# Attention logits written with their sign turned and a running minimum carried along, and the modulation rows placed under the last query tiles

## The chip, the cores and the metric

One core of a Trainium2 chip runs the whole kernel. The metric is the device time of one execution in microseconds (us), from the first to the last instruction with what lies around it. The engines are named as the profile names them: PE (matrix multiply) and PEld (its weight loads), DVE (the vector engine), ACT (the scalar engine), POOL (GpSimd) and SP (the queue that issues nearly all DMAs). Each engine works through its own queue in order.

## The reference, cut to what matters

One transformer block over 2048 tokens of width 1024. The change lies in the attention, which picks 256 keys for each query by a score and takes a softmax over them:

```
score = sum over 8 index heads of relu(qi . ki) * wi      # per query and key
idx   = top_k(score, 256)                                 # the threshold search
logits = (qa . ckv[idx]) * scale ;  p = softmax(logits) ;  ctx = p . ckv[idx]   # 8 heads
```

and in the modulation rows, which only the layers behind the attention need:

```
mod = silu(c) @ mod_w + mod_b      # c: 1 x 1024, mod_w: 1024 x 6144
sh1, sc1, g1, sh2, sc2, g2 = split(mod)
x = x + g1 * mix ;  h = rmsnorm(x) * (1 + sc2) + sh2 ;  x = x + g2 * moe(h)
```

## The kernel before

The kernel runs as stages: projections (to about 470 us of the profiled execution), attention (about 470 to 1157 us), the output product with the router, and the experts.

**Attention** (`attention`, from line 755) goes over 16 query tiles of 128 queries in the order written in `ORDER`: 0, 1, 2, 6, 7, ... 15, 5, 4, 3. I call them t0, t1, ... by the tile's own number. Tile t looks at (t+1)*128 keys. `p` is the place in that order: p = 4 is t7, p = 10 is t13, p = 12 is t15, p = 13 is t5. A tile has four groups g of two heads. For every (tile, group) `weave` interleaves five generators: `context` of this group (transposes of the exponentials, L1051, and products with the values, L1038), `logits` of the next group (L1012 to L1018), `scores` of the tile three places on (L846 to L850), and the `threshold` searches of the tiles one and two places on (L906 to L954). t5, t4 and t3 have nothing three places on, so the scores end with the work of p = 12. Behind this emission a list scheduler sets each engine's final order, so what stands on an engine is read from the built program.

**Logits** (L1002 to L1018 before): for one head the keys are cut in blocks of 512; PE makes a block in a PSUM bank (`pl`, three buffers), DVE adds the mask while it copies it out to `L` and writes the block's maximum to a column of `st` (one custom instruction and a small read of the accumulator, both L1013). When all blocks of the head are out, a DVE reduction over the one to four maxima gives the negated maximum (L1017), and ACT takes the exponential with it as bias (L1018). `st` is called `ast` in the profile.

**Modulation rows** (`modrows`, from line 169) are 64 steps of DVE work, one 128x512 piece of `mod_w` each, 256 KB, loaded by SP into a tile with two buffers:

```
w = mp.tile([128, 512], F32, name="modr", tag="modr", bufs=2)
with self.tc.issue_after(self.last.ins):
    nc.sync.dma_start(w, self.a["mod_w"][0, k * 128:(k + 1) * 128, o:o + 512])
if k == 0:
    nc.vector.tensor_scalar(acc, w, self.cond[:, 0:1], None, op0=OP.mult)          # L180
else:
    nc.vector.scalar_tensor_tensor(acc, w, self.cond[:, k:k + 1], acc, ...)        # L182
yield
```

`self.last` is the latest load of queries or keys, so a piece is issued behind it on SP. After every eighth piece come a product with ones on PE (L187, into a `pl` bank), an addition (L188) and a small store; that step yields too, so there are 72 steps. A piece's load can only be issued when the DVE step two pieces earlier has given its buffer back. `advance(rows, n)` takes n steps after a (tile, group), at a lowered priority. The layers behind the attention read the rows back from DRAM.

Of the kernel before, what the change touches and what calls it, by code (L numbers as in the profile page):

```python
# [15 lines left out]
AF = mybir.ActivationFunctionType  # L16
OP = mybir.AluOpType
AX = mybir.AxisListType
# [29 lines left out]
class K:  # L48
# [706 lines left out]
    def attention(self):  # L755
        nc, tc = self.nc, self.tc
        with ExitStack() as c1:
            ap = self.ap = c1.enter_context(tc.tile_pool(name="att", bufs=1, reuse_waits="tile"))
            self.pa = c1.enter_context(tc.tile_pool(name="pa", bufs=1, reuse_waits="tile", space=PSUM))
            self.exps = {}  # L760
            rows = self.modrows(ap)
            order = self.ORDER
            groups = [(t, g) for t in order for g in range(4)]
            thr = {}

            def scores(i):

                if i < NT and order[i] >= 3:
                    t = order[i]
                    S = self.ats.tile([128, T], F32, name="S", tag="S", bufs=3)  # L770
                    thr[i] = self.threshold(t, S)
                    return self.scores(t, S), 8 * -(-(t + 1) // 4)
                return iter(()), 0

            def bound(i):

                if i < NT and order[i] < 2:
                    self.plain(order[i])
                return thr.get(i, iter(()))
            for _ in bound(0), bound(1):  # L780
                pass
            for _ in self.logits(*groups[0]):
                pass
            for i, (t, g) in enumerate(groups):
                p = i // 4
                if g == 0:
                    sc, ns = scores(p + 3)
                    b1 = bound(p + 1) if p else iter(())
                    b2 = bound(p + 2)
                na = 2 * -(-(groups[i + 1][0] + 1) // 4) + 1 if i + 1 < len(groups) else 0  # L790
                nx = self.logits(*groups[i + 1]) if na else iter(())
                if g == 3:
                    for _ in b1:
                        pass
                self.weave((self.context(t, g), -(-(t + 1) // 2) + 1 + (g == 3)), (nx, na), (sc, ns // 4 + (g < ns % 4)),
                           (b1, 2), (b2, 1 + g % 2))
                if p >= 4:
                    with tc.high_priority(offset=-100):
                        self.advance(rows, 2)
                if g == 3:  # L800
                    self.advance(sc, 1000)
            for _ in rows:
                pass
            mix = [self.ats.tile([128, KT, 256], F32R, name="S", tag="S", bufs=3) for _ in range(2)]
            self.mix0 = self.mixed(0, mix, [ap.tile([128, 512], F32R, name="rel", tag="rel", bufs=3) for _ in range(2)],
                                   ap.tile([128, 4, 256], F32, name="cj", tag="cj", bufs=2),
                                   lambda: self.bank("pi", 2, (128, 2, 256)))
            self.W = [self.w_cut(self.w_load(k, ap), self.ats, *tag) for k, tag in enumerate((("S", 3), ("R", 1)))]
            raw = [self.w_load(k, ap) for k in range(2, 4)]
            self.repair()  # L810
            self.W += [self.w_cut(w, self.ats, "L", self.LB) for w in raw]
# [176 lines left out]
    def logits(self, t, g):  # L988

        nc, ap = self.nc, self.ap  # L990
        n = (t + 1) * 128
        bias = self.masks[t]
        c, o = t // 4, (t % 4) * 128
        if g == 0:
            self.st = ap.tile([128, 64], F32, name="ast", tag="ast", bufs=2)
        st = self.st
        q = ap.tile([128, 2, 2, 128], F32R, name="qa", tag="qa", bufs=3)
        for r in (slice(0, 64), slice(64, 128)):
            self.last = nc.sync.dma_start(q[r].bitcast(F32), self.qa_d[c][:, g, :, :, o:o + 128])
        P = [self.ats.tile([128, T], F32, name="L", tag="L", bufs=self.LB) for _ in range(2)]  # L1000
        self.exps[t, g] = P, st
        nb = -(-n // 512)  # L1002
        for h in (2 * g, 2 * g + 1):
            L = P[h % 2]
            k = ap.tile([128, T], F32R, name="kc", tag="kc", bufs=3)
            self.last = nc.sync.dma_start(k[:, :n].bitcast(F32), self.kh_d[g][h % 2].rearrange("l d t -> (l d) t")[:, :n])
            mx = st[:, 4 * h:4 * h + nb]
            for i, s in enumerate(range(0, n, 512)):
                e = min(s + 512, n)
                ps = self.bank("pl", 3)  # L1010
                for m in range(2):
                    nc.tensor.matmul(ps[:, :e - s], q[:, h % 2, m], k[:, s:e], start=m == 0, stop=m == 1)  # L1012
                nc.vector.tensor_tensor_reduce(L[:, s:e], ps[:, :e - s], bias[:, s:e], 1.0, -3e38,  # L1013
                                               OP.add, OP.max, mx[:, i:i + 1])
                yield
            neg = st[:, 32 + h:33 + h]
            nc.vector.tensor_reduce(neg, mx, axis=AX.X, op=OP.max, negate=True)  # L1017
            nc.scalar.activation(L[:, :n], L[:, :n], AF.Exp, bias=neg, accum_out=st[:, 40 + h:41 + h])  # L1018

    LB = 4  # L1020

# [791 lines left out]
```

## Time and profile before

| | |
|---|---|
| median of 3 runs | 2235.54 us (2231.49 to 2246.32) |
| the profiled execution | 2253.14 us, its span 2251.3 us |
| mean granted TensorE clock in it | 0.954 |
| busy in it: PE, DVE, ACT, POOL | 2007.1, 1611.3, 1219.2, 906.3 us |
| attention, first logits to the last tile's output | 470 to 1157 us |

The profiled execution took 0.8% longer than the median of the timed runs. Busy time is summed over stages with different limits; what the change touches is read in the attention alone, tile by tile. A tile's end is the DVE instruction at L1070 that writes its output.

### The profile page before, as it was taken

How to read it: one execution, taken by the hardware profiler on the slowest of the kernel's cores; microseconds unless marked ns; L12 is line 12 of the kernel's file. 1: busy time of each engine (PE TensorE's matmuls, PEld its weight loads, DVE VectorE, ACT ScalarE, POOL GpSimd, SP SyncE). 2: the span in 40 equal slices, each digit the busy share in tenths (PEclk: the TensorE clock that was granted, in tenths of full speed). 3: DMA queues.
4: the chain of work that ended last, by engine and by line, in shares of the span. 5: the costliest groups of instructions: out<-in, count | busy, mean ns of one | idle time of the engine just before them, and what ended most of it. 6: DMA issues, size and time to landing. Idle time of an engine off the chain costs nothing. (4 is left out here: it accounts for less than half of the span.)

```text
span 2251.3 us, 37139 instructions
## 1 busy us (share of the span) xinstructions
PE 2007.1 (89%) x12583; PEld 1509.5 (67%) x12584; DVE 1611.3 (72%) x3064; ACT 1219.2 (54%) x2026; POOL 906.3 (40%) x1586
## 2 busy tenths in 40 slices
PE   5899999987888999888979997699999999999983
PEld 4777887855666776776767785466776666666762
DVE  5696899678899989887435555567776676766583
ACT  4832332267777877776642221455665565655552
POOL 4542112537555434375000112334554554555343
PEclk9999999998999999999999998799999999999997
DMA  8737979865777766778877436599999999999894
GB/s 287 261 118 233 275 222 288 265 191 169 240 222 244 232 210 223 223 233 280 235 217 258 144 129 219 177 321 332 349 310 312 292 351 318 340 319 318 302 321 142
DMA packets 317038, 569.61 MB, mean 253 GB/s; under 512 B 35041, under 2 KB 148114, under 8 KB 315812
## 3 DMA queue, kind: packets, MB, share of 16 engines
q1 hardware_dynamic: 292068, 489.26, 66.1%
q0 software_dynamic: 22304, 68.41, 10.6%
q10 hardware_dynamic: 2464, 9.44, 1.1%
q8 instruction: 103, 1.69, 0.3%
q14 instruction: 99, 0.81, 0.1%
HBM read 462.44 MB, written 103.53 MB: 251 GB/s over the span
## 5 line engine op out<-in xcount | busy, mean ns | idle before, releaser
L1645 DVE TENSOR_TENSOR wl<-wr,wh 128x1024 fp32r<-128x1024 f32 x314 | 393.1, 1289 | 173.1 <-ACT wh L1644 172.3
L1644 ACT ACTIVATE wh<-wr 128x1024 fp32r<-128x1024 f32 x372 | 373.7, 1053 | 248.6 <-PE acc L94 182.9
L93 PE MATMUL acc<-wl,xh 128*128 128x512 f32 (+3 forms) x544 | 218.7, 403 | 5.4 <-POOL wl L1645 3.5
L92 PE MATMUL acc<-wh,xh 128*128 128x512 f32 (+3 forms) x544 | 215.9, 407 | 6.7 <-ACT wh L1644 5.0
L1013 DVE CUSTOM_DVE_ANT_0 L<-pl,bias 128x512 f32<-128x512 f32 (+3 forms) x312 | 180.8, 605 | 51.0 <-PE pt L1051 25.5
L94 PE MATMUL acc<-wh,xl 128*128 128x512 f32 (+3 forms) x544 | 215.6, 400 | 0.0
L1012 PE MATMUL pl<-kc,qa 128*128 128x512 f32 (+3 forms) x640 | 188.6, 398 | 25.3 <-DVE ast L1013 12.2
L1051 PE MATMUL pt<-identr,L 128*128 128x128 f32 x1088 | 174.6, 286 | 25.3 <-ACT pT L1053 19.0
L1053 ACT ACTIVATE pT<-pt 128x512 f32<-128x512 f32 (+1 forms) x288 | 158.4, 576 | 64.6 <-PE pt L1051 63.7
L849 ACT ACTIVATE rel<-pi 128x512 f32<-128x512 f32 (+3 forms) x296 | 155.5, 549 | 49.8 <-PE pi L847 23.2
L1645 POOL TENSOR_TENSOR wl<-wr,wh 128x1024 fp32r<-128x1024 f32 x58 | 145.7, 2560 | 90.9 <-ACT wh L1644 88.2
L850 DVE SCALAR_TENSOR_TENSOR S<-rel,wi,S 128x512 f32<-128x512 f32 (+3 forms) x259 | 171.3, 680 | 9.5 <-ACT rel L849 9.3
L611 DVE SCALAR_TENSOR_TENSOR ac<-u,kc,ac 128x512 f32<-128x512 f32 x240 | 175.4, 772 | 0.1
L1051 PEld LDWEIGHTS pt<-identr,L 128*128 128x128 f32 x1088 | 127.5, 144 | 69.4 <-ACT pT L1053 31.1
L1018 ACT ACTIVATE L<-L,ast 128x128 f32<-128x128 f32 (+15 forms) x128 | 154.2, 1207 | 18.5 <-DVE ast L1017 18.1
L1038 PE MATMUL po<-pT,vc 128*64 128x128 f32 x2176 | 150.7, 287 | 7.1 <-ACT pT L1053 6.8
L846 PE MATMUL pi<-kk,qi 128*128 128x512 f32 (+3 forms) x296 | 129.7, 440 | 27.4 <-ACT rel L849 27.0
L1038 PEld LDWEIGHTS po<-pT,vc 128*64 128x64 f32 x2176 | 124.7, 142 | 36.7 <-ACT pT L1053 17.8
L1012 PEld LDWEIGHTS pl<-kc,qa 128*128 128x128 f32 x640 | 110.6, 198 | 57.1 <-DVE ast L1013 24.7
L1695 POOL DMA_INDIRECT x_d<-yo,ent x32 | 93.1, 2910 | 92.6 <-DVE yo L1738 70.6
L92 PEld LDWEIGHTS acc<-wh,xh 128*128 128x128 f32 (+3 forms) x544 | 97.6, 182 | 43.8 <-ACT wh L1644 10.4
L93 PEld LDWEIGHTS acc<-wl,xh 128*128 128x128 f32 (+3 forms) x544 | 99.2, 182 | 37.3 <-POOL wl L1645 4.3
(525 smaller groups left out, 4688.7 us busy)
## 6 DMA issues: line engine op xcount, KB each, us to landing
wr<-in_exp_w_dram SPq DMA_DIRECT2D x256, 512.0 KB
wr<-in_exp_w_dram SPq DMA_DIRECT2D x64, 1024.0 KB
h<-h_d SPq DMA_DIRECT2D x64, 512.0 KB
vc<-v_d SPq DMA_DIRECT2D x112, 256.0 KB
h_d<-h POOLq DMA_DIRECT2D x32, 512.0 KB
qa<-qa_d SPq DMA_DIRECT2D x128, 128.0 KB
modr<-in_mod_w_dram SPq DMA_DIRECT2D x64, 256.0 KB
xt<-in_x_dram SPq DMA_DIRECT2D x16, 512.0 KB
```

The costliest lines, as they stand in the source:

```text
L92: mm(out, lh, rh, start=start, stop=False)
L93: mm(out, lh, rl, start=False, stop=False)
L94: mm(out, ll, rh, start=False, stop=stop)
L611: nc.vector.scalar_tensor_tensor(acc[j], src, kc[:, j, i:i + 1], acc[j], op0=OP.mult, op1=OP.add)
L850: nc.vector.scalar_tensor_tensor(S[:, s:e], r[:, :e - s], self.wi[:, t, h:h + 1], S[:, s:e] if h else self.tie[:, s:e], op0=OP.mult, op1=O ...
L1012: nc.tensor.matmul(ps[:, :e - s], q[:, h % 2, m], k[:, s:e], start=m == 0, stop=m == 1)
L1013: nc.vector.tensor_tensor_reduce(L[:, s:e], ps[:, :e - s], bias[:, s:e], 1.0, -3e38, OP.add, OP.max, mx[:, i:i + 1])
L1038: nc.tensor.matmul(po[r], v[:, (k2 + i) % 4, r], pT[:, i, j], start=len(left) > 2 * t, stop=len(left) <= 2)
L1051: nc.tensor.transpose(pt[:, i, j], P[j][:, (k2 + i) * 128:(k2 + i + 1) * 128], self.ident)
L1053: nc.scalar.activation(pT[:, :m], pt[:, :m], AF.Copy)
L1644: nc.scalar.activation(H[:, s], W[:, s], AF.Copy)
L1645: (nc.gpsimd if pool else nc.vector).tensor_tensor(L[:, s], W[:, s], H[:, s].bitcast(F32), OP.subtract)
```

## The change

Two edits. In `logits`, a block is written negated (factor -1), each block's minimum is started from the column of the block before in place of a constant, and so the last column holds the negated maximum of all the head's blocks; the reduction at L1017 is gone and the exponential turns the sign back with its scale. In `attention`, the modulation rows start at p = 10 (t13) in place of p = 4 (t7), with five steps after each group in place of two: 72 steps over 15 groups in place of 36.

```diff
-                if p >= 4:
+                if p >= 10:
                     with tc.high_priority(offset=-100):
-                        self.advance(rows, 2)
+                        self.advance(rows, 5)
...
-            mx = st[:, 4 * h:4 * h + nb]
             for i, s in enumerate(range(0, n, 512)):
                 e = min(s + 512, n)
                 ps = self.bank("pl", 3)
                 for m in range(2):
                     nc.tensor.matmul(ps[:, :e - s], q[:, h % 2, m], k[:, s:e], start=m == 0, stop=m == 1)
-                nc.vector.tensor_tensor_reduce(L[:, s:e], ps[:, :e - s], bias[:, s:e], 1.0, -3e38,
-                                               OP.add, OP.max, mx[:, i:i + 1])
+                low = st[:, 4 * h + i:4 * h + i + 1]
+                nc.vector.tensor_tensor_reduce(L[:, s:e], ps[:, :e - s], bias[:, s:e], -1.0,
+                                               st[:, 4 * h + i - 1:4 * h + i] if i else 3e38,
+                                               OP.add, OP.min, low)
                 yield
-            neg = st[:, 32 + h:33 + h]
-            nc.vector.tensor_reduce(neg, mx, axis=AX.X, op=OP.max, negate=True)
-            nc.scalar.activation(L[:, :n], L[:, :n], AF.Exp, bias=neg, accum_out=st[:, 40 + h:41 + h])
+            nc.scalar.activation(L[:, :n], L[:, :n], AF.Exp, scale=-1.0, bias=low, accum_out=st[:, 40 + h:41 + h])
```

The two edits also change what the scheduler puts where. Behind line 1007 the lines of the changed kernel are one lower (L1012 is L1011, L1070 is L1069); the DVE instruction of the logits is L1013 in both. The three places that the prediction speaks of follow.

DVE in the middle of the attention, in t8, before: the block of a head, the read of its accumulator (`ISA ast`), and the reduction L1017.

```order
L1013 ISA L,ast<-pl,bias 128x512 [waits PE_49]
L1013 ISA ast 128x1
L850 SCALAR_TENSOR_TENSOR S<-rel,wi,S 128x512 [waits Activation_49] x2
L950 SCALAR_TENSOR_TENSOR bias,sc<-S,sc,nbig 128x1280 [waits DVE_49]
L1017 TENSOR_REDUCE ast<-ast 128x1 [waits DVE_49]
L1013 ISA L,ast<-pl,bias 128x128 [waits PE_49]
L1013 ISA ast 128x1
```

The same engine at nearly the same place in the changed kernel:

```order
L1013 ISA L,ast<-pl,bias,ast 128x512 [waits DVE_49]
L1013 ISA ast 128x1
L1013 ISA L,ast<-pl,bias,ast 128x256 [waits DVE_49,PE_49]
L1013 ISA ast 128x1
L942 SCALAR_TENSOR_TENSOR R<-S,sc,R 128x1408 [waits Activation_49]
L1013 ISA L,ast<-pl,bias 128x512 [waits PE_49]
L1013 ISA ast 128x1
```

The reductions are gone, and a block after the first reads `ast` and waits for DVE itself, here right behind the read that writes it.

DVE in t15, before: pieces of the modulation rows (L182) between blocks of logits.

```order
L1013 ISA L,ast<-pl,bias 128x512
L1013 ISA ast 128x1
L947 TENSOR_TENSOR sc<-sc 128x1
L182 SCALAR_TENSOR_TENSOR macc<-modr,cond,macc 128x512 x2
L1013 ISA L,ast<-pl,bias 128x512
L1013 ISA ast 128x1
L1017 TENSOR_REDUCE ast<-ast 128x1
L1013 ISA L,ast<-pl,bias 128x512
L1013 ISA ast 128x1
L1013 ISA L,ast<-pl,bias 128x512
L1013 ISA ast 128x1
L1013 ISA L,ast<-pl,bias 128x512
```

The same engine in t15 in the changed kernel:

```order
L180 TENSOR_SCALAR macc<-modr,cond 128x512
L192 SCALAR_TENSOR_TENSOR mrow<-mrow,mg 1x512
L182 SCALAR_TENSOR_TENSOR macc<-modr,cond,macc 128x512
L1013 ISA L,ast<-pl,bias 128x512
L1013 ISA ast 128x1
L1013 ISA L,ast<-pl,bias,ast 128x512
L1013 ISA ast 128x1
L182 SCALAR_TENSOR_TENSOR macc<-modr,cond,macc 128x512
L1013 ISA L,ast<-pl,bias,ast 128x512
L1013 ISA ast 128x1
L182 SCALAR_TENSOR_TENSOR macc<-modr,cond,macc 128x512
L1013 ISA L,ast<-pl,bias,ast 128x512
```

Between the outputs of t14 and t15 stand 22 pieces in place of 5, often one or two blocks of logits apart.

SP at the start of t15's loads (rows of 2048 keys), before: keys (kc), values (vc), queries (qa) and the pieces (modr).

```order
L1006 DMA kc<-kh_d_71 128x2048 [waits DMAHW3_49,PE_49]
L178 DMA modr<-in_mod_w_dram 128x512 [waits DMAHW4_49,DVE_49]
L1006 DMA kc<-kh_d_72 128x2048 [waits DMAHW5_49,PE_49]
L999 DMA qa<-qa_d_70 64x4x128 [waits DMAHW6_49]
L999 DMA qa<-qa_d_70 64x4x128 [waits DMAHW7_49]
L1047 DMA vc<-v_d 128x512 [waits DMAHW0_49,PE_49]
L1047 DMA vc<-v_d 128x384 [waits DMAHW1_49,PE_49]
```

The same queue at the same loads in the changed kernel:

```order
L1006 DMA kc<-kh_d_71 128x2048 [waits PE_49]
L178 DMA modr<-in_mod_w_dram 128x512 [waits DMAHW7_49,DMAHW0_49,DVE_49]
L178 DMA modr<-in_mod_w_dram 128x512 [waits DMAHW3_49,DVE_49]
L1046 DMA vc<-v_d 128x512 [waits DMAHW1_49,PE_49]
L1046 DMA vc<-v_d 128x384 [waits DMAHW2_49,PE_49]
L178 DMA modr<-in_mod_w_dram 128x512 [waits DMAHW7_49,DVE_49]
L1006 DMA kc<-kh_d_72 128x2048 [waits DMAHW4_49,PE_49]
L178 DMA modr<-in_mod_w_dram 128x512 [waits DMAHW5_49,DMAHW0_49,DVE_49]
L999 DMA qa<-qa_d_70 64x4x128 [waits DMAHW6_49]
```

Four pieces stand where one stood, each with a wait for DVE, and the next keys and queries are queued behind them.

## Rows read from the trace of the kernel before

**Rows 1.** The page: span, busy time by engine, and the DMA issues of the pieces.
```profile
span 2251.3 us, 37139 instructions
...
PE 2007.1 (89%) x12583; PEld 1509.5 (67%) x12584; DVE 1611.3 (72%) x3064; ACT 1219.2 (54%) x2026; POOL 906.3 (40%) x1586
...
modr<-in_mod_w_dram SPq DMA_DIRECT2D x64, 256.0 KB
```

**Rows 2.** Windows by tile, t6 to t15, then t5: length, busy by engine, clock, DMA.
```profile
523.20:587.50 64.30, 49.72 (x300) 37.17 (x300) 54.38 (x138) 43.86 (x87) 38.33 (x131) 0.87 0.65 190
587.50:631.60 44.10, 36.96 (x269) 29.23 (x270) 35.79 (x88) 30.76 (x56) 24.69 (x78) 0.92 0.61 188
631.60:684.00 52.40, 45.50 (x331) 32.84 (x330) 47.50 (x121) 39.67 (x72) 27.45 (x78) 1.00 0.78 248
684.00:728.90 44.90, 41.44 (x335) 32.07 (x332) 42.10 (x102) 31.93 (x59) 24.56 (x73) 1.00 0.73 233
728.90:784.00 55.10, 50.83 (x384) 39.22 (x385) 49.38 (x115) 45.71 (x79) 24.68 (x76) 0.97 0.76 235
784.00:847.40 63.40, 58.24 (x419) 43.35 (x417) 54.81 (x124) 47.44 (x80) 23.91 (x67) 0.95 0.70 217
847.40:909.70 62.30, 56.93 (x433) 43.55 (x433) 58.10 (x134) 48.26 (x79) 28.59 (x79) 0.97 0.68 214
909.70:978.30 68.60, 60.02 (x477) 48.01 (x477) 60.48 (x144) 50.77 (x84) 32.29 (x115) 0.95 0.75 233
978.30:1044.60 66.30, 57.02 (x467) 44.79 (x465) 53.27 (x145) 48.45 (x80) 45.62 (x173) 0.95 0.73 233
1044.60:1097.40 52.80, 47.01 (x442) 37.10 (x442) 31.82 (x99) 36.99 (x56) 9.03 (x39) 0.97 0.86 276
1097.40:1121.40 24.00, 21.16 (x185) 16.94 (x183) 9.38 (x43) 15.21 (x31) 0.00 (x0) 0.93 0.88 235
```

**Rows 3.** Groups by form, attention: count, busy, mean ns of one, idle before.
```profile
L1013 DVE CUSTOM_DVE_ANT_0 L<-pl,bias 128x512 f32<-128x512 f32 x224 | 148.6, 684 | 40.4 <-PE pt L1051 25.5 <-PE pl L1012 14.5
...
L850 DVE SCALAR_TENSOR_TENSOR S<-rel,wi,S 128x512 f32<-128x512 f32 x196 | 144.2, 745 | 7.7 <-ACT rel L849 7.5
...
L182 DVE SCALAR_TENSOR_TENSOR macc<-modr,cond,macc 128x512 f32<-128x512 f32 x56 | 41.8, 747 | 22.0 <-DMA modr<-in_mod_w_dram 21.8
...
L1017 DVE TENSOR_REDUCE ast<-ast 128x1 f32<-128x4 f32 x32 | 4.8, 149 | 0.1
```

**Rows 4.** DVE timeline, one reduction: start, duration, instruction.
```profile
477.20 0.15 DVE L1017 TENSOR_REDUCE ast<-ast 128x1 f32<-128x1 f32 x1
477.26 0.61 DVE L850 SCALAR_TENSOR_TENSOR S<-rel,wi,S 128x384 f32<-128x384 f32 x1
```

**Rows 5.** DVE timeline, three small instructions, each reading the one before.
```profile
1077.92 0.15 DVE L952 TENSOR_SCALAR sc<-sc 128x1 f32<-128x1 f32 x1
1078.11 0.16 DVE L953 TENSOR_TENSOR sc<-sc 128x1 f32<-128x1 f32 x1
1078.31 0.15 DVE L954 TENSOR_SCALAR bad<-sc 128x1 f32<-128x1 f32 x1
```

**Rows 6.** Waits in the attention: who for whom, us, times, longest.
```profile
ACT L L1018 <- DVE ast L1017: 18.1, 27, 1.9
```

**Rows 7.** Timeline of pieces: SP's issue, DVE's step, in brackets its wait.
```profile
707.65 0.75 DVE L182 SCALAR_TENSOR_TENSOR macc<-modr,cond,macc 128x512 f32<-128x512 f32 x1 [0.25 <-DMA modr<-in_mod_w_dram]
...
713.33 0.85 SPq L178 DMA_DIRECT2D modr<-in_mod_w_dram  x2
720.43 0.75 DVE L182 SCALAR_TENSOR_TENSOR macc<-modr,cond,macc 128x512 f32<-128x512 f32 x1 [2.55 <-DMA modr<-in_mod_w_dram]
...
923.86 1.04 SPq L178 DMA_DIRECT2D modr<-in_mod_w_dram  x1
932.58 0.75 DVE L182 SCALAR_TENSOR_TENSOR macc<-modr,cond,macc 128x512 f32<-128x512 f32 x1 [2.83 <-DMA modr<-in_mod_w_dram]
...
1070.59 0.38 SPq L178 DMA_DIRECT2D modr<-in_mod_w_dram  x1
1075.06 0.75 DVE L182 SCALAR_TENSOR_TENSOR macc<-modr,cond,macc 128x512 f32<-128x512 f32 x1 [1.44 <-DMA modr<-in_mod_w_dram]
```

## The prediction

> **What bounds the kernel now.** I read the page first: PE is busy for 89% of the span and DVE for 72% [rows 1], which says little, since DVE's share is an average over stages. Then I cut the attention at the outputs of the tiles [rows 2]. There both are full: DVE 94% and PE 92% in t9, 90% and 92% in t10, 93% and 91% in t12. In t9 DVE has no time left at all: 42.10 us of work, and 0.25 + 2.55 us in which it stood waiting for a piece of the modulation rows [rows 7], make 44.9 of the window's 44.90 us. In t13 DVE is busy for 60.48 of 68.60 us, in t14 for 53.27 of 66.30. In t15 it falls to 31.82 of 52.80 us, because no scores are left to make. So DVE has room in t15, and the change moves work there. The third view is the timeline of the pieces, which shows how long a load takes from its issue on SP to the step on DVE that waited for it [rows 7].
>
> A measurement of this kernel tells about 1% (22 us) from no change.
>
> **The running minimum.** It removes 128 reductions, 32 of each of four forms, 149 ns each for the largest [rows 3]. Instructions overlap: the next one starts 0.06 us after a reduction [rows 4], so what DVE gets back is 128 x 0.06 = 8 us. It adds no instruction. It makes 192 of the 320 blocks (one per head in t4 to t7, two in t8 to t11, three in t12 to t15) read a column of `ast` that the block before wrote, and wait for it. In the changed order 25 of the 192 stand directly behind that write; for them the trace has three small instructions that each read the one before: they start 0.19 and 0.20 us apart [rows 5] where an independent one follows after 0.06 [rows 4], so 25 x 0.13 = 3 us. For the others the write is over long before. Reading a per-partition operand in place of a constant is not in the trace for this instruction. One bound is nothing; the other is the gap between L850, which has such an operand, and L1013, which has none, at 128x512: 745 - 684 = 61 ns, 192 x 0.061 = 12 us. I take the second, since it comes from the two rows most alike. The first edit's DVE sum is then -8 + 3 + 12 = +7 us, at best -5, spread over 13 tiles.
>
> The Trainium skill ("VectorE: DVE Perf Modes", The DRAIN you can't avoid) says that chained DVE instructions pay nothing for a semaphore, since the next one starts only when the pipe is empty anyway. Rows 4 and 5 differ: dependent small instructions stand 0.13 us further apart. By that rule the 3 us would be nothing.
>
> The exponential can now start one reduction earlier. ACT waited 18.1 us in 27 cases for that reduction [rows 6], but ACT is busy for only 71 to 83% in t8 to t14 [rows 2] and has slack, so I count no time for it; the far bound is a gain of 8 us if half of those waits held PE up. The -1 scale is an operand of an instruction that stays: nothing.
>
> **Pieces out of t6 to t12.** Between the outputs, the changed order has no piece in t6 to t11, 3 in t12, then 19, 16 and 22 in t13, t14 and t15 and 4 in t5. Before there were 7 in most tiles and 5 in t15. A step costs DVE 0.747 us by itself [rows 3], 0.66 from its start to the next one's. I counted the DVE rows of each tile in both orders, each at its distance to the next start in the trace. The difference per tile, moved threshold passes and reductions included, is t6 -7.3, t7 0, t8 -9.0, t9 -4.2, t10 -4.5, t11 -4.5, t12 +2.5, t13 +14.5, t14 -4.3, t15 +7.0, t5 +2.8 us. In t6 to t11 the waits for pieces go too, most of the 22.0 us of rows 3.
>
> What is late next there is PE. Its idle time in t6 to t11 is 324.2 - 282.7 = 41.5 us [rows 2], 14.6 of it in t6, 7.1 in t7, 6.9 in t8 and 3.5 to 5.2 in each of t9 to t11. At a PE share of 92%, the best of these tiles, t7 would give 3.9 us and t8 2.9, and t9 to t11 nothing; at 96% the sum over t7 to t11 is 17 us. The middle of the two is 12. t6 starts the pipeline of thresholds; at 96% it would give 12 us, and I take 4, since its wait is for that pipeline and not for pieces (3 of them). That makes **-16**, between -8 and -28. t12 takes three pieces and another threshold pass: +2.
>
> **Pieces into t13 to t15.** Here I forecast a loss, for two reasons.
>
> First, t13 becomes full. Its DVE work grows to 60.5 + 14.5 = 75 us, 19 pieces wait 22.0 / 56 = 0.39 us each [rows 3], 7.4 us, and 25 carried blocks cost 1.5: 84 us against 68.6. DVE works in order, so nothing shortens that: +15. In t14 work leaves: DVE falls to 49 us, PE loses 7 us of score products, and t14 becomes 61 in place of 66.3: -5.
>
> Second, two buffers set a pace. A piece can be issued when the step two before it is done. From issue to the waiting step it takes 4.5 us at the shortest and 8.7 at the longest [rows 7]; piece 713.33 took 7.1. I take the middle, 6.6. Two pieces then need 6.6 + 0.7 = 7.3 us. Before, the pieces came 6 to 9 us apart each, so this bound nothing. In t15 there are now 22, 11 pairs: 11 x 7.3 = **80 us against 52.8**, +27. While DVE stands at a piece, the blocks of logits behind it on DVE wait, PE waits for their three banks, and ACT for the exponentials. t14's 8 pairs need 58 us, within its 61. On SP the same pieces wait for DVE with the next keys, values and queries queued behind them. t15 moves 276 GB/s at a DMA share of 0.86 already [rows 2]; 17 more pieces of 256 KB [rows 1] are 4.5 MB, 16 us at that rate, so a shorter latency there is not to be expected. t5 takes the last four: +2, and the rows' products on PE (16 of them) move along at no net cost.
>
> The give-back is +2 + 15 - 5 + 27 + 2 = +41; with -16, **+25 us**. On the profiled execution that is 2253 + 25 = 2278, 1.1% more; on the median 2235.5 x 1.011 = **2260 us**.
>
> **The rivals.**
>
> *The loads land fast enough.* Issued more often, a piece may land as quickly as the shortest, 4.5 us; pairs need 5.2 us and t15 11 x 5.2 = 57: +4 in place of +27. t13's waits shrink by half, +11, and t14 keeps -8. The give-back is +2 + 11 - 8 + 4 = +9, the net -7: 2253 - 7 on the profiled execution, **2228 us** on the median. The point is where the give-back is 16: with t13 and t14 as here t15 may then take 64 us, 5.8 a pair, a latency of 5.1 us in t15; below that the kernel is not slower. For it: the shortest row is in t15 itself. Against it: that piece was issued alone, and pieces behind a load of keys took 6 to 9.
> The Trainium skill ("DMA: Bandwidth & Descriptors", Anatomy of one DMA) fits 2.0 us plus the bytes at 436 GB/s for loads issued from GpSimd: by that page 256 KB is an estimated 2.6 us, and the pace would bind nowhere. The rows of this case, issued from SP among other loads, show none under 4.5.
>
> *DVE's relief pays in full.* If DVE alone held t6 to t11 and the waits at pieces were on the path, the gain is 28 us, and with fast loads the net is -19: 2235.5 - 19 = **2216**, and some us lower if the exponentials' earlier start counts. For it: t9's account of DVE, full to the last 0.1 us. Against: at the same time PE is busy for 92%.
>
> *Both ends bad.* No gain beyond t7 and t8 (-8), the pace at 8 us a pair (t15 11 x 8 = 88, +35; t14 8 x 8 = 64, -2), SP held at pieces so that keys come late: +2 + 15 - 2 + 35 + 3 = +53, net +45: **2280 us**. For it: four pieces between the loads of two heads. PE idle may also cost clock: the lowest granted clock of rows 2 to t14, 0.87, a mean of its two levels of 1.2 and 2.4 GHz, stands beside the lowest PE share. That stays in the range.
>
> **How the numbers follow.** The forecast has a chance of 0.46, the fast loads 0.25, both ends bad 0.19, the full relief 0.10. The likeliest case alone spans 2246 to 2276 (latency 6 to 7.2, gain 10 to 22). The range of 8 in 10 leaves out most of the full relief and what lies beyond the bad case: 2222 to 2290. Slower by over 1% is above 2258: six tenths of the forecast, the bad case and a little, 0.49. Faster by over 1% is below 2213: the lower half of the full relief and a little of the fast loads, 0.08. Within 1% is the rest, 0.43.
>
> **What would show it.** In the changed profile the windows between outputs should show t8 and t7 shorter by some 3 to 5 us, t9 to t11 nearly as long, t13 near 84, t14 near 61 and t15 near 80. DVE's idle time at L182 behind `modr` should rise from 22 us to over 50, nearly all after the output of t12, with 6 to 8 us from issue to step. The reductions are gone from DVE and the 128x512 block stands at about 745 ns, or at 684 if the operand is free. I am wrong if t15 stays under 60 us: then the pace of two buffers was no limit. I am wrong in the other term if t6 to t11 lose more than 28 us.

## The result and the profile after

The changed kernel takes **2262.01 us** (median of 7 runs, 2255.51 to 2265.1) against 2235.54 (median of 7, 2231.49 to 2246.32): a ratio of **1.0108, 95% interval 1.0085 to 1.0131**. The forecast was 2260. Where the time went agrees with the forecast in some places, and for the first edit it does not; the experiments show which.

The windows of the changed kernel between the outputs of the tiles, t6 to t15 in turn, with the columns of [rows 2]:

```profile
527.05:583.67 56.62, 46.64 (x292) 35.80 (x292) 48.30 (x118) 39.57 (x79) 36.96 (x128) 0.88 0.59 170
583.67:624.57 40.90, 34.48 (x274) 28.31 (x275) 36.42 (x82) 34.58 (x65) 22.66 (x81) 0.98 0.72 214
624.57:671.26 46.69, 42.21 (x320) 32.40 (x319) 40.03 (x92) 37.41 (x67) 22.71 (x78) 0.98 0.65 204
671.26:716.30 45.04, 42.22 (x341) 33.29 (x341) 39.93 (x95) 34.98 (x64) 22.04 (x78) 1.00 0.66 204
716.30:767.86 51.56, 49.45 (x385) 38.72 (x383) 46.31 (x98) 44.62 (x82) 19.36 (x67) 1.00 0.69 215
767.86:823.81 55.95, 52.94 (x411) 40.92 (x409) 51.11 (x108) 47.04 (x79) 24.70 (x81) 1.00 0.65 199
823.81:895.46 71.65, 61.57 (x450) 47.09 (x448) 63.02 (x124) 53.20 (x88) 28.66 (x88) 0.95 0.60 192
895.46:983.91 88.45, 70.64 (x491) 53.82 (x491) 76.29 (x169) 58.07 (x98) 53.49 (x173) 0.88 0.68 207
983.91:1047.99 64.08, 53.80 (x437) 40.84 (x437) 50.76 (x134) 38.08 (x60) 33.41 (x131) 0.92 0.88 291
1047.99:1117.03 69.04, 55.04 (x458) 40.79 (x456) 40.85 (x96) 36.12 (x56) 0.00 (x0) 0.95 0.88 272
```

Against [rows 2], t6 to t11 are shorter by 27.4 us together, and t12 to t15 are longer by 9.4, 19.8, -2.2 and 16.2. With the small tiles the attention grows by 17.8 us (704.2 against 686.4 from the first logits to the last output), yet the two profiled executions differ by only 9: behind the attention the one of before took 9.7 us longer. Stretches of the stage behind it, before:

```profile
1256.10:1306.10 50.00, 47.66 (x416) 37.89 (x409) 25.03 (x57) 10.54 (x20) 7.43 (x9) 0.93 0.34 117
```

and after, as far behind its last output:

```profile
1274.70:1324.70 50.00, 50.00 (x490) 40.36 (x489) 30.07 (x65) 13.76 (x26) 9.43 (x11) 1.00 0.41 138
```

PE was granted 0.93 there before, a mean of its two levels 1.2 and 2.4 GHz, and 1.00 after, the upper level, in a stretch in which it was busy without a gap. The profiled execution of before, 2253.14 us, is longer than each of the kernel's 7 timed runs and than its 13 runs beside the first four experiments (2221.73 to 2248.64 us); it lies 17.6 us above the median, while the one after is the median itself. That is why the medians differ by more than the two profiles. Where the other executions of before save those 17.6 us isn't shown. Experiment 6, whose DVE order is that of before, was profiled in a long execution too (2253.5 us at a median of 2243.39), with nearly the same attention (682.8 us).

The logits and the pieces of the changed kernel, grouped by form:

```profile
L1013 DVE CUSTOM_DVE_ANT_0 L<-pl,bias,ast 128x512 f32<-128x512 f32 x120 | 89.4, 745 | 3.6 <-PE pl L1011 1.7
L1013 DVE CUSTOM_DVE_ANT_0 L<-pl,bias 128x512 f32<-128x512 f32 x104 | 70.5, 686 | 21.2 <-PE pt L1050 16.1 <-PE pl L1011 4.8
L182 DVE SCALAR_TENSOR_TENSOR macc<-modr,cond,macc 128x512 f32<-128x512 f32 x56 | 41.9, 749 | 30.2 <-DMA modr<-in_mod_w_dram 29.9
L188 DVE TENSOR_TENSOR mrow<-mrow,pl 1x512 f32<-1x512 f32 x8 | 5.4, 671 | 8.5 <-DMA mrow<-in_mod_b_dram 7.3 <-PE pl L187 1.2
L180 DVE TENSOR_SCALAR macc<-modr,cond 128x512 f32<-128x512 f32 x8 | 3.9, 490 | 10.6 <-DMA modr<-in_mod_w_dram 10.6
```

A block that reads the column takes 745 ns, one that doesn't 686. DVE waited 40.5 us for pieces (29.9 at L182 and 10.6 at L180), against 26.0 before (21.8 [rows 3] and 4.2), and once 7.3 us for the bias row behind them.

What DVE waits for in t15, after (us in total, times, longest):

```profile
DVE macc L182 <- DMA modr<-in_mod_w_dram: 12.0, 11, 2.8
DVE mrow L188 <- DMA mrow<-in_mod_b_dram: 7.3, 1, 7.3
DVE macc L180 <- DMA modr<-in_mod_w_dram: 6.8, 2, 5.0
```

And the pace of two buffers in the timeline of t15, first SP's issues of pieces, then DVE's steps (start, duration; in brackets the wait):

```profile
1075.55 0.33 SPq L178 DMA_DIRECT2D modr<-in_mod_w_dram  x1
1079.03 3.18 SPq L178 DMA_DIRECT2D modr<-in_mod_w_dram  x2
...
1074.77 0.75 DVE L182 SCALAR_TENSOR_TENSOR macc<-modr,cond,macc 128x512 f32<-128x512 f32 x1
1078.25 0.75 DVE L182 SCALAR_TENSOR_TENSOR macc<-modr,cond,macc 128x512 f32<-128x512 f32 x1 [1.15 <-DMA modr<-in_mod_w_dram]
1081.10 0.75 DVE L182 SCALAR_TENSOR_TENSOR macc<-modr,cond,macc 128x512 f32<-128x512 f32 x1 [2.10 <-DMA modr<-in_mod_w_dram]
1084.71 0.75 DVE L182 SCALAR_TENSOR_TENSOR macc<-modr,cond,macc 128x512 f32<-128x512 f32 x1 [0.66 <-DMA modr<-in_mod_w_dram]
```

The step at 1074.77 gives its buffer back, the next issue is at 1075.55, its step at 1081.10, 5.6 us later; the step at 1078.25, the issue at 1079.03, the step at 1084.71.

### The profile page after: what moved, and what is told of

It is laid out like the page before. It is cut to its first block, busy times and chain, and to the rows that moved or that the text cites. A ratio compares the mean times of both kernels' runs of the same rounds, so it can differ in the third digit from the quotient of the medians.

```text
span 2260.3 us, 37151 instructions
## 1 busy us (share of the span) xinstructions
PE 2004.4 (89%) x12583; PEld 1507.4 (67%) x12584; DVE 1618.5 (72%) x2936; ACT 1217.3 (54%) x2026; POOL 884.2 (39%) x1586
## 3 DMA queue, kind: packets, MB, share of 16 engines
q1 hardware_dynamic: 292068, 489.26, 65.7%
## 5 line engine op out<-in xcount | busy, mean ns | idle before, releaser
L1011 PE MATMUL pl<-kc,qa 128*128 128x512 f32 (+3 forms) x640 | 194.4, 402 | 30.0 <-DVE ast L1013 19.2
L850 DVE SCALAR_TENSOR_TENSOR S<-rel,wi,S 128x512 f32<-128x512 f32 (+3 forms) x259 | 171.0, 681 | 18.1 <-ACT rel L849 17.9
L1017 ACT ACTIVATE L<-L,ast 128x128 f32<-128x128 f32 (+15 forms) x128 | 154.3, 1207 | 40.9 <-DVE ast L1013 40.0
L1011 PEld LDWEIGHTS pl<-kc,qa 128*128 128x128 f32 x640 | 109.9, 199 | 64.8 <-DVE ast L1013 34.4
L1013 DVE CUSTOM_DVE_ANT_0 L<-pl,bias,ast 128x512 f32<-128x512 f32 (+3 forms) x192 | 123.3, 645 | 7.6 <-PE pl L1011 4.9
L92 PEld LDWEIGHTS acc<-wh,xh 128*128 128x128 f32 (+3 forms) x544 | 97.4, 182 | 43.8 <-ACT wh L1643 10.2
```

Source lines behind the costliest of these rows:

```text
L92: mm(out, lh, rh, start=start, stop=False)
L850: nc.vector.scalar_tensor_tensor(S[:, s:e], r[:, :e - s], self.wi[:, t, h:h + 1], S[:, s:e] if h else self.tie[:, s:e], op0=OP.mult, op1=O ...
```

## The experiments

P is the theory of the prediction: the place of the rows makes the loss. C puts it on the carried minimum, D on DVE's work and not the loads. Ratios are to the kernel before, in runs on the same chip.

**1. The carried minimum alone.** The kernel before with the second part of the diff only; the rows keep `if p >= 4` and two steps.

> The kernel before with the negated logits and the running minimum alone; the modulation rows stay where they were, from t7 on, two steps a group. Theory P (the place of the rows makes the loss): the operand read from a column costs 192 x 0.059 = 11 us of DVE and the 128 reductions give back 8, spread over 13 tiles in which DVE is not everywhere the last, so 2231 to 2244 us, ratio 0.998 to 1.004. Rival C (the carried minimum makes the loss, since blocks of one head now wait for one another): 2253 to 2263 us, ratio 1.008 to 1.012, and t12 and t13 long as in the changed kernel.

Measured: 2262.47 us, **1.0127 (1.0086 to 1.0167)**. P is wrong here, and C's time comes out (the ratio just over its range). But C's other sign, t12 and t13 as long as in the changed kernel, doesn't: they take 66.1 and 65.7 us (71.7 and 88.5 there). The stretch from t8 to t12 as one window, before:

```profile
631.57:909.71 278.14, 252.99 (x1898) 191.07 (x1896) 251.94 (x590) 213.03 (x368) 129.19 (x371) 0.98 0.73 228
```

with the carried minimum alone, t8 to t12, and then t14 and t15:

```profile
622.34:931.67 309.33, 268.79 (x1935) 204.22 (x1934) 278.64 (x588) 225.83 (x390) 141.65 (x415) 0.94 0.66 206
997.38:1117.22 119.84, 101.22 (x894) 80.13 (x893) 73.75 (x198) 76.42 (x119) 30.41 (x126) 0.94 0.81 254
```

Before, t14 and t15 took 66.30 + 52.80 = 119.1 us with 53.27 + 31.82 = 85.1 of DVE [rows 2]. Now DVE has 73.75 us there and they are no shorter, while t8 to t12 hold 26.7 us more DVE work and are 31.2 longer. The scores at L850 show the move: 10.08 us of DVE lay in t14 before and 3.73 now (DVE busy at L850 behind the comma; before, then with the carried minimum alone),

```profile
978.31:1044.61 66.30, 10.08 (x16) 0.95 0.73 233
997.38:1064.10 66.72, 3.73 (x5) 0.92 0.82 265
```

and in t8 to t12 they rose from 97.42 to 111.38 us. So work went from tiles where DVE has room into tiles where it is nearly full. Not all of the 26.7 us is moved work: t14 and t15 gave up 11.3 and t6 and t7 6.6, while DVE's work over t6 to t4 rose by 8.4.

**2. The rows alone.** The kernel before with `if p >= 10` and five steps.

> The kernel before with the rows moved alone (from t13 on, five steps a group); logits with constants and a reduction over the partial maxima, as before. Theory P: nearly the whole loss, ratio 1.007 to 1.012, 2251 to 2263 us; t6 to t11 some 25 to 30 us shorter, t13 and t15 each 14 to 20 us longer. Rival C: within 5 us of the kernel before, ratio 0.998 to 1.003.

Measured: 2265.27 us, **1.0149 (1.0107 to 1.0191)**, a little over P's range. t6 to t11 lost 22.8 us against [rows 2]; t13 to t15:

```profile
892.05:960.21 68.16, 58.82 (x460) 47.20 (x461) 59.93 (x141) 48.77 (x83) 24.35 (x82) 0.93 0.82 255
960.21:1036.49 76.28, 60.92 (x480) 46.82 (x478) 64.16 (x162) 49.11 (x81) 52.20 (x177) 0.95 0.79 255
1036.49:1106.20 69.71, 54.72 (x447) 40.47 (x448) 44.76 (x118) 36.01 (x57) 11.53 (x47) 0.90 0.85 263
```

t15 is 17 longer as said; t13 stays, against what was expected, and t14 takes 10 in its place. So by their ratios the edits cost 28 and 33 us alone, and 24 together.

**3. The changed kernel with four buffers.** `tag="modr", bufs=4`.

> The changed kernel with four buffers for the pieces of the rows in place of two. Theory P with the pace of two buffers: the waits at pieces in t15 (18.8 us in the changed kernel) shrink to a few us, t15 goes from 69 to about 57 and t14 from 64 to about 62: 12 to 16 us less than the changed kernel, 2246 to 2250 us, ratio to before 1.005 to 1.007. Rival D (the room on DVE and the blocks of logits behind the pieces set t13 to t15, not the loads): t15 stays at 66 or more, 2258 to 2266 us, ratio 1.010 to 1.014.

Measured: 2252.47 us, 1.009 (1.0055 to 1.0125). t15 by its window, and then DVE's waits in it:

```profile
1043.73:1100.74 57.01, 50.02 (x452) 38.58 (x450) 39.71 (x92) 35.37 (x55) 0.00 (x0) 0.97 1.01 331
```

```profile
DVE macc L182 <- DMA modr<-in_mod_w_dram: 6.2, 6, 1.6
DVE macc L180 <- DMA modr<-in_mod_w_dram: 4.9, 2, 3.9
```

t15 is 57.0 where 57 was expected: 12 of its 16 us belonged to the two buffers, and t13 to t15 together are 12.9 shorter (208.7 against 221.6), so the time didn't just move to a neighbour. 11.1 us of waits remain, in a window whose DMA engines were busy throughout (share 1.01, 331 GB/s). The whole time lies between P's range and D's, and its gain over the changed kernel within the interval.

**4. The changed kernel with one piece loaded.** The load at L178 only for the first piece:

```diff
-                w = mp.tile([128, 512], F32, name="modr", tag="modr", bufs=2)
-                with self.tc.issue_after(self.last.ins):
-                    nc.sync.dma_start(w, ...)
+                if i == k == 0:
+                    w = mp.tile([128, 512], F32, name="modr", tag="modr", bufs=1)
+                    with self.tc.issue_after(self.last.ins):
+                        nc.sync.dma_start(w, ...)
```

> The changed kernel with one single piece of mod_w loaded and read by all 64 steps: leaves out 63 of the 64 loads, so the rows are not those of the reference, and all work of DVE and PE stays. Theory P: the waits at pieces (40.5 us in 30 cases in the changed kernel) are gone; those on the way to the end are t15's 18.8 and part of t13's and t14's 14: 16 to 26 us less than the changed kernel, 2236 to 2246 us, ratio to before 1.000 to 1.005; t15 at 52 to 56. Rival D: no more than 8 us less, 2254 to 2262 us, ratio 1.008 to 1.012.

Its whole time, 2522.32 us (1.1289, 1.1244 to 1.1334), can't be read, since the layers behind the attention work on other rows. t13 to t15:

```profile
896.74:986.89 90.15, 71.91 (x482) 54.90 (x482) 78.28 (x175) 55.36 (x94) 55.09 (x165) 0.85 0.46 147
986.89:1058.61 71.72, 58.25 (x454) 44.31 (x453) 56.66 (x142) 42.68 (x67) 37.08 (x140) 0.90 0.73 228
1058.61:1107.70 49.09, 46.66 (x446) 36.59 (x446) 34.87 (x86) 34.31 (x53) 0.00 (x0) 1.00 0.76 233
```

Together 211.0 us against 221.6 in the changed kernel: all loads cost 10.6 us there, less than P said and more than D. t13 is no shorter without the loads, so they don't set its length. What does isn't settled: DVE is busy for 78.28 of its 90.15 us and PE for 71.91, at a granted clock of 0.85.

**5. The operand without the chain.** Blocks after the first start from a column that always holds 3e38, and the reduction stays, as a minimum:

```diff
-                                               OP.add, OP.max, mx[:, i:i + 1])
+                                               self.top if i else 3e38, OP.add, OP.min, low)
```

> The kernel before with negated logits whose 192 later blocks start their minimum from a column that always holds 3e38, and with the reductions (as minima) kept: the price of the operand without the chain from block to block. In the built program the scores and threshold passes that DVE makes during t14 and t15 stay there (27.4 thousand columns of them against 24.7 before; 13.6 with the carried minimum alone). Theory M (the chain makes the scheduler put scores and thresholds ahead of the blocks, out of t14 and t15, where DVE has room, into t8 to t12, where it has none): only the operand is left, 192 x 0.059 = 11 us of DVE, part of it on the way to the end: 2233 to 2245 us, ratio 1.001 to 1.006; t8 to t12 together within 12 us of before. Rival O (the operand's price itself, in tiles where DVE is full): 2252 to 2264 us, ratio 1.009 to 1.015, t8 to t12 some 30 us longer.

Measured: 2247.19 us, **1.0011 (0.9997 to 1.0026)**; t8 to t12:

```profile
630.47:907.29 276.82, 249.61 (x1889) 189.40 (x1889) 252.83 (x587) 210.88 (x364) 122.18 (x366) 0.98 0.73 230
```

The operand costs 59 ns, and hardly any time: rival O falls, as to the operand.

**6. Negated blocks alone.** The same with the constant 3e38 for every block.

> The kernel before with negated blocks, minima from a constant and the reduction kept as a minimum: no chain, no operand. DVE's order in the built program is the one of the kernel before, row for row in its scores, threshold passes and pieces. All theories: no change, ratio 0.996 to 1.004. Its profile is a second look at the order of before, whose first profiled execution was some 17 us above its median.

Measured: 2243.39 us, 0.9998 (0.9982 to 1.0013). Its profile shows t8 to t12 as the kernel before does:

```profile
628.70:905.73 277.03, 251.91 (x1898) 190.21 (x1896) 251.68 (x589) 212.53 (x368) 130.81 (x371) 0.98 0.73 227
```

**7. The kernel before with four buffers.**

> The kernel before with four buffers for the pieces in place of two, DVE's order unchanged. The 22 us in which DVE stood at L182 should go to under 5. Theory M and P: DVE is full in t9 and nearly so in t8, t10 and t12, where about half of those waits lie, so 5 to 12 us faster than before, ratio 0.994 to 0.998, 2219 to 2227 us. Rival D (the pieces' loads are hidden in the kernel before, PE sets the end there): ratio 0.998 to 1.002.

Measured: 2240.37 us, **0.9978 (0.9961 to 0.9995)**. The time is at the edge of what was expected and the reason is wrong: the waits stay. Where the 0.2% comes from isn't shown.

```profile
L182 DVE SCALAR_TENSOR_TENSOR macc<-modr,cond,macc 128x512 f32<-128x512 f32 x56 | 41.9, 748 | 20.3 <-DMA modr<-in_mod_w_dram 20.3
```

Where the pieces stand far apart, the buffers don't set the waits.

**8. The rows alone with four buffers.**

> The kernel before with the rows moved (from t13 on, five steps a group) and four buffers. Theory P: against the rows moved with two buffers t15, t5 and t4 lose their waits (some 12 + 4 + 3 us), so 2244 to 2250 us, ratio 1.004 to 1.010; t15 at 54 to 58. Rival D: no more than 6 us less than with two buffers, 2259 to 2265 us.

Measured: 2253.36 us, **1.004 (1.0025 to 1.0055)**, against 1.0149 with two: the direction and the ratio of P. But it isn't shorter where P said. t15 took 67.2 us and not 54 to 58, though DVE's waits at pieces in it fell from 24.2 us (experiment 2) to 10.2. The window of t15, and two of DVE's waits in it:

```profile
1034.60:1101.83 67.23, 50.36 (x438) 39.63 (x437) 42.99 (x115) 35.48 (x58) 12.56 (x43) 0.90 0.82 257
```

```profile
DVE macc L182 <- DMA modr<-in_mod_w_dram: 9.5, 5, 4.7
DVE cj L906 <- POOL sc L924: 5.4, 2, 2.9
```

A threshold search is still at work in t15 here (1.5 us of DVE at L906, none in experiment 3), and DVE waits for its steps on POOL. So with the logits of before the pace of two buffers is hardly t15's limit; in the order of the changed kernel it is.

**9. The carried minimum with the two heads in turn.** Experiment 1, with the loop over blocks outside and the one over heads inside, so that a block reads a column written two blocks earlier; both exponentials follow at the end.

```diff
-        for h in (2 * g, 2 * g + 1):
...
-            for i, s in enumerate(range(0, n, 512)):
+        for i, s in enumerate(range(0, n, 512)):
+            for h in (2 * g, 2 * g + 1):
```

> The kernel before with the carried minimum, and the blocks of the two heads of a group emitted in turn, so that a block reads the column written two blocks earlier; rows as before. In the built program DVE keeps during t14 and t15 as many columns of scores and threshold passes as before (9.7 and 15.0 thousand), where the carried minimum alone kept 5.6 and 7.9. Theory M (the chain between neighbouring blocks lets the scheduler pull that work forward into full tiles): the loss of the carried minimum alone goes, ratio 0.995 to 1.004. Rival O (the carried minimum costs by itself: operand, chain, serial blocks): 1.008 to 1.014.

Measured: 2256.73 us, **1.0091 (1.0073 to 1.011)**: theory M misses, and the time is in rival O's range. The late work stayed, as t14's scores show (10.26 us of DVE at L850, 10.08 before); t8 to t12 as one window:

```profile
619.26:912.03 292.77, 262.71 (x1915) 198.02 (x1915) 261.75 (x562) 217.04 (x374) 136.30 (x404) 0.96 0.71 219
```

Still 10 us more DVE work and 16 us more time than in experiment 6, and t13 and t15 are 6 to 7 longer. Whether that is the chain or the two heads in turn, the run can't say: the turn also takes the keys of both heads at once and puts both exponentials last, and the turn without the chain wasn't run.

**10. The carried minimum with the reductions kept.**

> The kernel before with the carried minimum and, on top, the reductions kept (as minima over the columns); rows as before. In the built program still less is left on DVE for t14 and t15: 3.1 thousand columns of scores and 5.4 of threshold passes. Theory M: at least the loss of the carried minimum alone plus the 8 us of the reductions, ratio 1.012 to 1.022; t8 to t12 together 30 us or more longer than before. Rival R (the missing reductions change the order and make the loss): ratio under 1.006.

Measured: 2272.77 us, **1.0163 (1.0143 to 1.0183)**. t8 to t12, then t12 and t14:

```profile
627.40:953.97 326.57, 275.64 (x1967) 209.06 (x1966) 289.71 (x641) 235.31 (x405) 151.40 (x444) 0.94 0.64 202
870.63:953.97 83.34, 68.06 (x488) 52.50 (x487) 72.04 (x157) 59.26 (x100) 38.34 (x112) 0.92 0.62 197
1022.81:1074.17 51.36, 44.79 (x420) 35.20 (x421) 36.68 (x103) 35.07 (x54) 12.91 (x58) 1.00 0.93 303
```

The chain makes the loss with the reductions there too (R falls): t12 takes 14 us more DVE work than in [rows 2] and is 21 longer, t14 gives 17 back and is 15 shorter.

**11. The changed kernel with the heads in turn.**

> The changed kernel (carried minimum, rows from t13 on, two buffers) with the blocks of the two heads in turn. Theory M says why the two edits cost 28 and 33 us alone and 27 together: the chain empties t14 and t15 of scores and thresholds, which makes room there for the pieces. With the heads in turn that work stays in t14 and t15 and meets the pieces: no faster than the changed kernel, ratio 1.008 to 1.016, t13 under 80 but t14 over 70 and t15 about 69. Rival A (the costs add, the heads in turn take the chain's part away): 1.000 to 1.005.

Measured: 2274.16 us, **1.017 (1.0147 to 1.0194)**: with experiment 10 the slowest, experiment 4 aside, and a little over M's range; A falls. t13 to t15:

```profile
899.48:973.48 74.00, 63.54 (x469) 48.32 (x470) 64.91 (x139) 50.69 (x86) 30.83 (x98) 0.92 0.72 228
973.48:1047.38 73.90, 59.85 (x465) 44.80 (x465) 60.48 (x144) 46.59 (x76) 47.52 (x166) 0.92 0.83 249
1047.38:1117.15 69.77, 51.91 (x444) 39.17 (x443) 45.76 (x112) 37.88 (x59) 15.53 (x57) 0.93 0.85 267
```

t14 holds 60.48 us of DVE where the changed kernel holds 50.76, and is 10 longer.

**12. The candidate.** Experiment 9 with four buffers.

> The candidate: carried minimum, heads in turn, rows placed as before with four buffers. If both small gains hold (no reductions, some 8 us of DVE less against 11 for the operand; four buffers 0.2 %), ratio 0.993 to 1.001; by rival O 1.006 to 1.012.

Measured: 2251.92 us, 1.0072 (1.0052 to 1.0092). That is in rival O's range and not in the first one. It is ahead of the changed kernel (1.0108), with intervals that just overlap, and behind the one before. The only version clearly ahead of the one before is experiment 7, by 0.2%.

## Why the prediction was right, point by point

The time came out as forecast, 2262 against 2260, and part of that is luck. The sum for t6 to t15 has the right sign, but is +15.8 us where the terms give -16 + 2 + 15 - 5 + 27 = +23, and on the profiled execution, from which the forecast was worked out, it said 2278 where 2262 was measured. The medians differ by more than the profiles because the profiled execution of before was a long one. The share of the two edits in the loss did not come out at all.

**t6 to t11: -16 forecast, -27.4 measured**, at the end of its bounds (-8 to -28). I took PE as the limit with its 282.7 us of busy time fixed, and that failed: it fell to 267.9, with nearly as many instructions (2023 against 2038), while the granted clock of t7, t10 and t11 rose from 0.92, 0.97 and 0.95 to 0.98, 1.00 and 1.00. t9 alone behaves as argued (+0.1); t6 (-7.7) and t11 (-7.5) gave more than I allowed. The rival that DVE's relief pays in full had 28 us for these tiles.

**t12: +2 forecast, +9.4.** Mis-sized: DVE has 63.0 us there against 58.1 [rows 2], +4.9. My count of DVE's rows gave +2.5 us, and PE's work, which grew from 56.9 to 61.6 with the scores that come forward, I had not counted.

**t13: +15 forecast, +19.8.** The DVE work was right (75 against 76.3), and so was the size of its waits at pieces (7.4 against 8.7). But that they make the length is wrong: experiment 4 has none and takes 90.2 us.

**t14: -5 forecast, -2.2.** PE's work fell by 3.2 us (57.0 to 53.8) and not by 7.

**t15: +27 forecast, +16.2.** The mechanism is shown for this kernel: with four buffers t15 loses 12 of the 16 (with the logits of before it hardly shows, experiment 8). The size was off: I took 6.6 us from issue to step. That is the mean (6.65) of the 17 steps that waited before; the 13 that waited in t15 now had 3.0 to 10.1 us, 5.3 in the mean. A pair took 69.04 / 11 = 6.3 us in place of 7.3. Of the announced signs t13 near 84 and blocks of 745 ns came (88.4; 745), while DVE's idle time at L182 rose to 29.9 us and not to over 50. t5 didn't grow at all.

**The first edit: +7 us of DVE forecast, and no more.** DVE work over t6 to t4 rose by 8.4 us (513.3 against 504.9, by the windows of all tiles), the block with an operand stands at 745 ns as taken, and the adjacent dependents cost 4.7 us of waiting where I had 3 (below). But its effect on the time, alone, is 28 us, and I had it at nothing beyond that. What I left out is that a wait between neighbouring blocks changes what the scheduler puts ahead of them. By the Trainium skill's page "VectorE: DVE Perf Modes" (The DRAIN you can't avoid) a semaphore between chained DVE instructions costs nothing extra; the trace doesn't agree, with 0.11 to 0.25 us for each such wait. Neither price comes near 28 us. Experiment 5 has the operand without the chain and costs 0.1%, so the cost came with the chain.

**Why the sign still held.** I worked from the changed kernel's real order, so the moved work was in my counts tile by tile, under the name of the rows. The two edits also seem to cover for each other. The chain takes scores and thresholds out of t14 and t15 into t8 to t12; the rows leave t8 to t12 and go to t13 to t15. In the changed kernel each goes where the other has made room: t8 to t12 take 270.9 us with 240.4 of DVE. Experiment 11 undoes the first move and keeps the second, and is slower than the changed kernel (1.017 against 1.0108). That fits, but doesn't prove it, since the heads in turn cost 0.9% in experiment 9 too.

**What the windows of t8 to t12 say.** Five kernels, and DVE's share of that stretch is nearly the same: 0.906 before, 0.913 (operand), 0.901 (carried minimum), 0.894 (heads in turn), 0.887 (with reductions), while it lasts from 276.8 to 326.6 us. PE's share falls from 0.910 before to 0.844 in the longest. So where work is added there, the time follows DVE's work. Where work is taken out, DVE's share falls as well and PE's rises a little: 0.861 and 0.921 with the rows alone, 0.887 and 0.917 in the changed kernel. This is read from shares; no run holds PE fixed.

**What stays open.** The carried minimum alone costs 28 us. Experiments 5, 6 and 10 leave only the chain; that the scheduler then pulls work forward is shown in 1 and 10; that this is the whole loss isn't, since experiment 9 left the late work in its place and still lost 20 us.

**Slips in the working.** The operand stands in twelve tiles, t4 to t15, and not in 13. The latencies and gains named for the likeliest case give about 2248 to 2274 us, not 2246 to 2276, and the rival of fast loads leaves out the 2 us of t5. None of them moves the forecast.

## What to carry to other kernels

A dependence between neighbouring instructions of a busy engine costs little on the engine and may cost much in the schedule: count each engine's work per stage in both programs, and look whether it moved from a stage with room into a full one. Loads that are brought together need buffers for their new spacing; two were enough at one piece in 6 to 9 us (experiment 7) and not at one in 3 (experiment 3). Two edits that each lose can lose less together than their sum (28 and 33 us, and 24), so test them alone and together.

## What the runs showed of the hardware

A block that reads the column which the instruction just ahead has written starts 0.11 us after the start of that read of the accumulator. In the timeline of DVE in the changed kernel's t15:

```profile
1082.38 0.08 DVE L1013 DVE_READ_ACCUMULATOR2_ANT ast<- 128x1 f32 x1
1082.49 0.75 DVE L1013 CUSTOM_DVE_ANT_0 L<-pl,bias,ast 128x512 f32<-128x512 f32 x1
```

A block without the column starts together with the read (at 1086.44 both); the next one, which has a second semaphore to wait for and a semaphore instruction of its own on DVE's queue, starts 0.22 us after the read:

```profile
1086.44 0.08 DVE L1013 DVE_READ_ACCUMULATOR2_ANT ast<- 128x1 f32 x1
1086.44 0.68 DVE L1013 CUSTOM_DVE_ANT_0 L<-pl,bias 128x512 f32<-128x512 f32 x1
1087.06 0.08 DVE L1013 DVE_READ_ACCUMULATOR2_ANT ast<- 128x1 f32 x1
1087.28 0.75 DVE L1013 CUSTOM_DVE_ANT_0 L<-pl,bias,ast 128x512 f32<-128x512 f32 x1
```

In the changed kernel 5 blocks show the 0.11 to 0.12 us and 18 the 0.22 to 0.25, 4.7 us in all. In experiment 5, whose column no block writes, 83 of the 87 such blocks right behind a read start with it.

From issue to step the 13 pieces of t15 that DVE waited for took 3.0 to 10.1 us, 5.3 in the mean, against 4.5 to 8.7 and 6.65 in the mean for the 17 of the kernel before, at nearly the same rate in t15 (272 GB/s, 276 before). So with 22 pieces in the tile in place of 5 they were not slower; the prediction had expected no shorter latency. The Trainium skill's page "DMA: Bandwidth & Descriptors" (Anatomy of one DMA) has a fit for loads issued from GpSimd, by which such a piece is an estimated 2.6 us. These are issued from SP among other loads; the shortest comes near that, most don't.
